# A gated recurrence with its products regrouped: gates and queries transposed by the matmul, values beside the attention's keys, both head pairs in one pass

## The chip, the cores and the metric

The kernel runs on one core of a Trainium2 chip. TensorE (PE in the profile) multiplies matrices out of SBUF into PSUM banks; VectorE (DVE) and ScalarE (ACT) do the elementwise work; GpSimd (POOL) does a little; SyncE (SP) issues most DMAs. The metric is the device time of one execution in microseconds (us); lower is better.

## The reference, cut to what matters

The network is two transformer blocks in fp32 on 256 tokens `x` (and, in the first block, 256 context tokens `ctx`). The first block has two layers, `l = 0` and `l = 1`; each mixes its tokens by a Fourier mix, an attention and the gated recurrence of this change, from one projection `u = h @ w_in`, and then has a feed-forward part. Layer 0 gives outputs for both sequences; layer 1 gives outputs for `x` alone, but still needs the recurrence's states after `ctx`. The recurrence runs forward (gate columns `OFF_FF`) and backward (`OFF_FB`), in chunks of 64 tokens, with 4 heads of 64:

```python
k = (1 - lb) * sigmoid(-z);  log_f = log(lb + (1 - lb) * sigmoid(z))     # per direction
def step(s, inp):                                                        # one chunk
    kc, vc, lf, qc = inp
    cum = cumsum(lf);  last = cum[-1]
    s_new = exp(last) * s + einsum('sd,se->de', kc * exp(last - cum), vc)
    o_inter = einsum('td,de->te', qc * exp(cum), s)
    att = einsum('td,sd,tsd->ts', qc, kc, exp(cum_t - cum_s) where s <= t)
    return s_new, o_inter + einsum('ts,se->te', att, vc)
...
y = rmsnorm(o_forward + o_backward, gain) * silu(g)
```

The second block (windowed and dilated attention, feed-forward) is not touched by the change.

## The kernel before, in words

**Products.** A product in fp32 is made from three fast ones: each operand is split into a high part (`hi`, line 170, on ACT) and the rest (`lo`, line 171, on DVE), and `mm3` issues hi·hi, hi·lo and lo·hi (lines 177 to 179). The weights come by DMA in chunks of two k-tiles (`raw`), and are split into `whi` and `wlo`. `gemm` keeps the activations stationary and streams the weights, so its result has tokens on partitions. `gemm_t` keeps the weights stationary and streams 512 tokens, so its result has columns on partitions, i.e. transposed; `gemm_t2` does this for 256 tokens.

**The recurrence in `mix1`.** The four heads are two pairs, `fd` 0 and 1. `z_(fd)` makes 512 columns for one pair by `gemm`: 128 each of forward gate, backward gate, values and queries, which `hg_load` collects from four places of `w_in` in pieces of 128 columns. The result is copied to `zn`. In layer 1 the context tokens take 384 of the columns (no queries), and `z_(0)` is made in two gemms, for `ctx` and for `x`, each with its own loading and splitting of the weights. `h_(seq, fd)` then does a sequence of 256 tokens (four chunks) for one pair, in one call of `fwd`:

- `hgrn_gates`: PE transposes the gates (line 1102, four transposes) and the queries (line 1115, two) into PSUM; sigmoids from there (lines 1106 and 1107, ACT); products of query and gate (DVE).
- `hgrn_levels`: the attention within a chunk is built in levels of block size 1, 2, 4, ..., 32, after a group for the diagonal. A level copies halves of `hxy` into `hkm` (lines 1184 and 1186, ACT), multiplies 64x64 blocks (line 1156, PE; the profile counts 16 for one pair), and puts the result under a mask into `hatt` (line 1167, `copy_predicated`, DVE). Then DVE multiplies the gates of the level into `hxy` (lines 1202 and 1203), which the next level's copies wait for. So there are 7 groups for a sequence and a pair with queries. A pass without queries (`ctx` in layer 1) has none of these groups.
- `hgrn_states`: transposes of the keys (line 1222), products with the values (line 1235), the running states `hst` (line 1251), and their copies `hsb` (line 1264).
- `hgrn_out`: products of queries with states and of `hatt` with values (lines 1283 and 1293).

Tiles of a pass have two buffers each (`hbufs = 2`). `k_` makes the attention's keys and values, 256 columns for all tokens; `q_`, `g_` and `u_` make queries, the output gate and the Fourier part; `e_` ends a pool; `r_` normalises the recurrence's output; `a_` is the attention. `STEPS` gives the order in which these are written, one string for each layer. A scheduler merges the written instructions into one list per engine, so that a gemm's matmuls lie between the small steps of the recurrence. The first product of layer 0 is started while the norm still runs (`start` in `run`), as its chunks arrive.

Of the kernel before, what the change touches and what calls it, by code (L numbers as in the profile page):

```python
# [12 lines left out]
F32 = mybir.dt.float32  # L13
# [18 lines left out]
    "z0 h00 z1 g h01 e k h10 h11 q u m a r",  # L32
    "z0 h00 h10 z1 e h01 k h11 q g u m a r",
# [61 lines left out]
class Net:  # L95
    def __init__(self, ctx, tc, A, out, taps=None, stop=None):
# [16 lines left out]
        self.hbufs = 2  # L113
# [613 lines left out]
    def gemm_t(self, xT, w, n0, nb, first=False):  # L727


        xh, xl = xT  # L730
# [20 lines left out]
        return acc  # L751
# [336 lines left out]
    def hgrn_gates(self, pool, zn, seq, fds, l, with_q):  # L1088


        nc, nf = self.nc, len(fds)
        f = self.t(pool, [P, 2 * nf, 256], F32, "hf", bufs=self.hbufs)
        xy = self.t(pool, [P, 4 * nf, 256], F32, "hxy", bufs=self.hbufs)
        q = self.t(pool, [P, 2 * nf, 256], F32, "hq", bufs=self.hbufs) if with_q else None
        ends = xy.rearrange("p (s j) t -> p s j t", s=4)[:, 0::3]
        for i in range(2):
            ts = slice(i * P, i * P + P)
            ps = self.tr_bank()
            for j, fd in enumerate(fds):
                for d in range(2):  # L1100
                    o = (d * nf + j) * P
# [253 lines left out]
    def mix1(self, hp, pool, l, hT, start=None, late=None):  # L1355
# [61 lines left out]
        def h_(seq, fd):  # L1417
            with_q = seq in seqs
            now = nexts == f"h{seq}1"
            if now:  # L1420
                obank(seq)
# [493 lines left out]
```

## Time and profile before

| what | value |
|---|---|
| median of 3 runs | 1678.8 us (1677.87 to 1680.21) |
| profiled execution: time | 1683.74 us |
| profiled execution: span | 1681.9 us |
| granted TensorE clock, mean over the span | 0.989 |
| busy share of the span | PE 96%, weight loads 80%, DVE 73%, ACT 51%, POOL 3% |
| DMA | 310.48 MB, mean 185 GB/s |
| chain that ended last, by engine | PE 71%, DVE 10%, DMA 10%, ACT 5%, issue 3% |

The span is the profiled execution without the time around it (1683.74 - 1681.9 = 1.8 us). The recurrence of layer 0 lies in the stretch from 23 to 200 us, that of layer 1 between 700 and 820 us. The chain is followed back from the last instruction; a share of PE in it is time for which nothing but PE's own work was waited for. A busy PE counts overlapping matmuls once, so the cost of a matmul is read from the start of one to the start of the next.

### The profile page before, as it was taken

The page shows a single profiled execution, that of the slowest core. Times are in us where ns is not written, and L with a number is a line of the kernel's source. Part 1 is how long each engine was busy: PE and PEld are TensorE (multiplying, and loading weights), DVE is VectorE, ACT ScalarE, POOL GpSimd, SP SyncE. Part 2 cuts the span into 40 slices and gives each one's busy share as a digit, 9 for nine tenths or more (in the row PEclk, how much of TensorE's full clock was granted, in tenths as well). Part 3 has the DMA queues.
Part 4 walks back from the last instruction along what each step waited for, and adds up shares of the span by engine and source line. Part 5 has one row for each costly group of instructions (what it writes and reads, how often), then busy time and mean ns, then how long its engine had stood idle before and what let it go on. Part 6 is the DMA issues. An engine that isn't in the chain of part 4 may idle for free.

```text
span 1681.9 us, 27316 instructions
## 1 busy us (share of the span) xinstructions
PE 1621.6 (96%) x10343; PEld 1344.0 (80%) x10343; DVE 1222.3 (73%) x2042; ACT 855.5 (51%) x1697; POOL 44.6 (3%) x53
## 2 busy tenths in 40 slices
PE   7999899999999999999999999999999999899998
PEld 5777757878888888787678899777989988779896
DVE  4558866887878977878768897887776567575555
ACT  4446664533333234554755455686454456564443
POOL 0001100000000000101000000000000000000000
PEclk9999999999999999999999999999999999999999
DMA  9550415554678886532258897533876543256653
GB/s 325 187 176 27 161 64 188 176 189 165 212 231 297 271 265 222 161 90 70 91 187 295 309 315 253 158 119 119 275 260 188 185 135 90 85 176 173 206 175 112
DMA packets 169482, 310.48 MB, mean 185 GB/s; under 512 B 12163, under 2 KB 72819, under 8 KB 169350
## 3 DMA queue, kind: packets, MB, share of 16 engines
q1 hardware_dynamic: 168966, 308.17, 56.8%
q8 instruction: 81, 1.33, 0.3%
q10 hardware_dynamic: 384, 0.56, 0.1%
q14 instruction: 51, 0.42, 0.1%
HBM read 307.64 MB, written 1.05 MB: 184 GB/s over the span
## 4 chain that ended last, share of the span: by engine, by line
PE 71%; DVE 10%; DMA 10%; ACT 5%; issue 3%; POOL 1%; SPq 1%; ACTq 0%; POOLq 0%; DVEq 0%
PE bank L179 19%; PE bank L177 19%; PE bank L178 19%; DVE wlo L171 3%; ACT whi L170 3%; PE bank L970 2%; PE bank L897 2%; DMA raw<-ffn_w_in 2%; DMA raw<-w_up 2%; DMA raw<-w_down 2%; DMA raw<-w_gate 1%; PE bank L1512 1%; PE bank L321 1%; DMA raw<-ffn_w_out 1%; PE bank L1156 1%
## 5 line engine op out<-in xcount | busy, mean ns | idle before, releaser
L170 ACT CAST whi<-raw 128x1024 fp32r<-128x1024 f32 (+2 forms) x420 | 401.1, 959 | 525.4 <-PE bank L179 186.6
L171 DVE TENSOR_TENSOR wlo<-raw,whi 128x1024 fp32r<-128x1024 f32 (+2 forms) x420 | 464.7, 1111 | 239.2 <-ACT whi L170 237.2
L177 PE MATMUL bank<-hh,whi 128*128 128x256 f32 (+1 forms) x1240 | 385.4, 311 | 0.0
L178 PE MATMUL bank<-hl,whi 128*128 128x256 f32 (+1 forms) x1240 | 384.8, 311 | 0.0
L179 PE MATMUL bank<-hh,wlo 128*128 128x256 f32 (+1 forms) x1240 | 384.3, 311 | 0.4 <-DVE wlo L171 0.2
L177 PE MATMUL bank<-whi,hh 128*128 128x512 f32 (+2 forms) x720 | 266.8, 374 | 11.0 <-ACT hh L170 5.8
L178 PE MATMUL bank<-wlo,hh 128*128 128x512 f32 (+2 forms) x720 | 265.5, 369 | 2.1 <-DVE wlo L171 2.1
L179 PE MATMUL bank<-whi,hl 128*128 128x512 f32 (+2 forms) x720 | 263.8, 370 | 0.2 <-DVE hl L171 0.2
L179 PEld LDWEIGHTS bank<-hh,wlo 128*128 128x128 f32 x1240 | 233.3, 188 | 16.0 <-DVE wlo L171 1.0
L178 PEld LDWEIGHTS bank<-hl,whi 128*128 128x128 f32 x1240 | 233.7, 188 | 14.8
L177 PEld LDWEIGHTS bank<-hh,whi 128*128 128x128 f32 x1240 | 233.6, 188 | 14.9
L358 DVE SCALAR_TENSOR_TENSOR acc<-adaw,cs,acc 128x1024 f32<-128x1024 f32 x154 | 196.4, 1281 | 20.0 <-DMA adaw<-ada_w 10.8
L178 PE MATMUL bank<-wlo,acth 128*128 128x512 f32 x440 | 173.6, 394 | 0.5 <-DVE wlo L171 0.5
L177 PE MATMUL bank<-whi,acth 128*128 128x512 f32 x440 | 173.3, 394 | 0.0
L179 PE MATMUL bank<-whi,actl 128*128 128x512 f32 x440 | 172.6, 392 | 0.0
L177 PEld LDWEIGHTS bank<-whi,hh 128*128 128x128 f32 x720 | 138.0, 193 | 38.7 <-ACT hh L170 8.0
L179 PEld LDWEIGHTS bank<-whi,hl 128*128 128x128 f32 x720 | 138.5, 192 | 23.7 <-DVE hl L171 3.7
L178 PEld LDWEIGHTS bank<-wlo,hh 128*128 128x128 f32 x720 | 138.6, 193 | 21.9 <-DVE wlo L171 3.4
L177 PEld LDWEIGHTS bank<-whi,acth 128*128 128x128 f32 x440 | 82.7, 188 | 18.8 <-DVE sg L840 0.4
L179 PEld LDWEIGHTS bank<-whi,actl 128*128 128x128 f32 x440 | 82.8, 188 | 18.7
L178 PEld LDWEIGHTS bank<-wlo,acth 128*128 128x128 f32 x440 | 82.7, 188 | 18.7 <-DVE wlo L171 0.9
L756 DVE TENSOR_TENSOR rtmp<-bank,gate 128x512 f32<-128x512 f32 x68 | 46.6, 686 | 32.3 <-PE bank L179 32.3
(297 smaller groups left out, 1834.7 us busy)
## 6 DMA issues: line engine op xcount, KB each, us to landing
adaw<-ada_w SPq DMA_DIRECT2D x96, 512.0 KB
adaw<-w_ada SPq DMA_DIRECT2D x80, 512.0 KB
raw<-ffn_w_in SPq DMA_DIRECT2D x64, 512.0 KB
raw<-w_down SPq DMA_DIRECT2D x46, 512.0 KB
raw<-ffn_w_out SPq DMA_DIRECT2D x40, 512.0 KB
raw<-w_gate SPq DMA_DIRECT2D x32, 512.0 KB
raw<-w_up SPq DMA_DIRECT2D x32, 512.0 KB
raw<-w_in SPq DMA_DIRECT2D x56, 256.0 KB
```

Source lines behind the costliest of these rows:

```text
L170: a = self.nc.scalar.copy(hi, src)
L171: b = self.nc.vector.tensor_sub(lo, src, hi.bitcast(F32))
L177: mm(out, lh, rh, start=start, stop=False)
L178: mm(out, lh, rl, start=False, stop=False)
L179: mm(out, ll, rh, start=False, stop=stop)
L321: nc.tensor.matmul(ps[h][32 * g : 32 * g + 32], self.cs32[:, k0 + g], raws[g][:, h * 512 : h * 512 + 512], start=k0 == 0, stop=k0 > 0,)
L358: nc.vector.scalar_tensor_tensor(acc, raw, s, acc, op0=ALU.mult, op1=ALU.add)
L756: nc.vector.tensor_mul(tmp[:, :nw], ps[:, :nw], gate[:, n0 : n0 + nw])
L897: self.nc.tensor.transpose(ps[:, i * P : i * P + P], ps_in[:, i * P : i * P + P], self.ident)
L970: self.nc.tensor.matmul(o[e * 64 : e * 64 + 64], v, pt[:, e::2, i], start=i == 0, stop=i == len(vs) - 1)
L1156: nc.tensor.matmul(banks[hp][(c % 2) * 64 : (c % 2) * 64 + 64, 2 * j + c // 2], lhs(hs, j, c), rhs(hs, j, c), start=True, stop=True,)
L1512: nc.tensor.matmul(dst, q, ksT[:, i, kv, :nk], start=i == 0, stop=i == 1)
```

## The change

The 512 gate columns of both pairs become one `gemm_t` (`f_`), and the 256 query columns another (`y_`; in layer 1 a `gemm_t2` for `x` alone). Both come out transposed, in `zf` and `zq`, so that the transposes of `hgrn_gates` go. The values join the attention's keys and values in one gemm of 512 columns (`v_`, result `zv`). `hgrn_gates`, `hgrn_levels`, `hgrn_states` and `hgrn_out` now always take both pairs (`nf = 2`), so that an instruction of a level has twice the elements and a group of 64x64 products has 32 instead of 16. The pass is cut in two steps: `L_(seq)` is gates and levels, `S_(seq)` is states and outputs, and other work may be written between them. The tiles of a pass have one buffer (`hbufs = 1`). Line numbers shift: line 1156 becomes 1147, 1167 becomes 1158, 1184 and 1186 become 1175 and 1177, 1202 and 1203 become 1193 and 1194.

```diff
 STEPS = (
-    "z0 h00 z1 g h01 e k h10 h11 q u m a r",
-    "z0 h00 h10 z1 e h01 k h11 q g u m a r",
+    "f y L0 g e v S0 L1 q S1 u m a r",
+    "f L0 e v y S0 L1 q g u S1 m a r",
 )
...
-        self.hbufs = 2
+        self.hbufs = 1
...
+    def gemm_t_steps(self, xT, w, n0, nb, first=False, ahead=0):
...
-    def hgrn_gates(self, pool, zn, seq, fds, l, with_q):
-
-
-        nc, nf = self.nc, len(fds)
+    def hgrn_gates(self, pool, z, qv, l):
+
+
+
+        nc, nf, fds = self.nc, 2, (0, 1)
         f = self.t(pool, [P, 2 * nf, 256], F32, "hf", bufs=self.hbufs)
         xy = self.t(pool, [P, 4 * nf, 256], F32, "hxy", bufs=self.hbufs)
...
-                    nc.tensor.transpose(
-                        ps[:, o : o + P], zn[fd][:, 2 * seq + i, d * P : d * P + P], self.ident
-                    )
...
+        nc.scalar.activation(f, z, AF.Sigmoid)
+        nc.scalar.activation(
+            ends, z.rearrange("p (d j) t -> p d j t", d=2), AF.Sigmoid, scale=-1.0
+        )
...
-    def hg_load(self, l, fd, m):
...
+        def f_():
+
+            z_["f"] = z = self.t(pool, [P, 4, 512], F32, "zf", bufs=1)
+            if start is None:
+                acc = self.gemm_t(hT, w, 1024, 4, first=True)
+            else:
+                *_, acc = start
+            for i, a in enumerate(acc):
+                self.copy(z[:, i], a)
+
+        def y_():
+
+            z_["q"] = z = self.t(pool, [P, 2, 512 if ctx_out else 256], F32, "zq", bufs=1)
+            if ctx_out:
+                for i, a in enumerate(self.gemm_t(hT, w, 1792, 2)):
+                    self.copy(z[:, i], a)
+            else:
+                (a,) = self.gemm_t2(self.sides(hT)[1], w, 1792, 2)
+                self.copy(z, a.rearrange("p (j t) -> p j t", j=2))
...
+        def L_(seq):
+            q = None
+            if seq in seqs:
+                q = z_["q"][:, :, 256 * seq : 256 * seq + 256] if ctx_out else z_["q"]
+            z = z_["f"][:, :, 256 * seq : 256 * seq + 256]
+            f, xy, ks = self.hgrn_gates(hg, z, q, l)
+            att, last = self.hgrn_levels(hg, f, xy, q, ks)
+            kept[seq] = xy, att, last
+
+        def S_(seq):
+            xy, att, last = kept.pop(seq)
+            out = seq in seqs
+            self.hgrn_states(hg, xy, last, z_["v"], seq, states, sbs if out else None)
+            if out:
+                o = self.ac_bank()
                 osb[seq] = self.t(pool, [P, 512], F32, "osb", bufs=len(seqs))
...
-        def k_():
+        def v_():
...
-            acc = self.gemm(hT, range(KT), w, 0, 768, 256, allt)
+            wv = w[:, 768:].rearrange("k (m c) -> k m c", m=2)
+            load = lambda dst, k: nc.sync.dma_start(
+                out=dst.rearrange("p (m c) -> p m c", m=2), in_=wv[k : k + P, :, :256]
+            )
+            acc = self.gemm(hT, range(KT), load, 0, 0, 512, allt)
             for i, a in enumerate(acc):
+                self.copy(zv[:, i], a[:, 256:])
+                self.copy(v[:, i], a[:, 128:256])
...
-            start = self.gemm_steps(
-                hT, range(KT), self.hg_load(0, 0, 4), 0, 0, 512, [0, 128, 256, 384], ahead=1, early=True
-            )
+            start = self.gemm_t_steps(hT, A["w_in"][0], 1024, 4, ahead=1)
```

The first place is PE in layer 1, in the levels of the `x` tokens. Before, three groups of line 1156 stand there with no gemm's matmul between them (each group has its own `hkm`):

```order
L177 MATMUL bank_1514_7932<-whi_7936,hh_6416 128x256
...
L1156 MATMUL bank_1462_7621<-hkm_7617 64x64
...
L1156 MATMUL bank_1465_7640<-hkm_7636 64x64 x4
...
L1156 MATMUL bank_1468_7659<-hkm_7655 64x64
...
L178 MATMUL bank_1483_7797<-wlo_7838,hh_6416 128x512
```

Now four groups of the doubled size (line 1147) stand together, between a matmul with `whi` of a gemm of 256 columns and the one with its `wlo`; each group has 16 of these rows, of which one stands here:

```order
L179 MATMUL bank_1390_7405<-whi_7408,hl_6158 128x256
...
L177 MATMUL bank_1390_7405<-whi_7426,hh_6157 128x256
L1147 MATMUL bank_1346_7164<-hkm_7160 64x64
...
L1147 MATMUL bank_1349_7191<-hkm_7187 64x64
...
L1147 MATMUL bank_1352_7218<-hkm_7214 64x64
...
L1147 MATMUL bank_1355_7245<-hkm_7241 64x64 x3
...
L1213 MATMUL bank_1419_7560<-ident_73,hxy_7069 128x128 x4
L178 MATMUL bank_1389_7404<-wlo_7427,hh_6157 128x256
```

What moved is the gemm work: it stands before and behind the four groups, and one more group, each of 32 instead of 16 products by the profile's count, is in the row.

The second place is DVE in layer 0, in the first two levels of the first pass. Before (`h00`, one pair):

```order
L1202 TENSOR_TENSOR hxy_616<-hxy_616,hf_615 128x256
L1203 TENSOR_TENSOR hxy_616<-hxy_616,hf_615 128x256
L1167 COPY_PREDICATED hatt_636<-mask_546,bank_150_653 128x128
...
L1202 TENSOR_TENSOR hxy_616<-hxy_616,hlev_635 128x128x2
L1203 TENSOR_TENSOR hxy_616<-hxy_616,hlev_635 128x128x2
```

Now (`L0`, both pairs):

```order
L1193 TENSOR_TENSOR hxy_719<-hxy_719,hf_718 128x512
L1194 TENSOR_TENSOR hxy_719<-hxy_719,hf_718 128x512
L1158 COPY_PREDICATED hatt_727<-mask_542,bank_174_752 128x256
...
L1193 TENSOR_TENSOR hxy_719<-hxy_719,hlev_726 128x256x2
L1194 TENSOR_TENSOR hxy_719<-hxy_719,hlev_726 128x256x2
L171 TENSOR_TENSOR wlo_948<-raw_945,whi_947 128x512
```

The kinds and their order are the same; each has twice the elements, and there are half as many of them in a layer.

The third place is ACT in layer 0 between the states of `ctx` (step `S0`) and the levels of `x` (`L1`), in the changed kernel. `hsb` are the states' copies, and the sigmoid into `hxy` writes the one buffer that the outputs of `S0` read:

```order
L1255 COPY hsb_578<-hst_576 64x2x3x64 x2
L1107 ACT_TABLE_LOAD
L1107 ACTIVATE hxy_1463<-zf_582 128x2x512
L1411 COPY osb_1420<-bank_282_1419 128x512
L1175 COPY hkm_1492<-hxy_1463 128x512
L1177 COPY hkm_1492<-hxy_1463 128x256 x2
```

On PE, the last output products of `S0` (line 1284) and the first group of `L1` (line 1147) stand there so:

```order
L1284 MATMUL bank_282_1419<-zv_1123,hatt_727 64x64 x16
L178 MATMUL bank_312_1657<-wlo_1693,hh_112 128x512
L179 MATMUL bank_312_1657<-whi_1692,hl_113 128x512
L177 MATMUL bank_313_1658<-whi_1692,hh_112 128x512
...
L177 MATMUL bank_314_1659<-whi_1692,hh_112 128x512
L178 MATMUL bank_314_1659<-wlo_1693,hh_112 128x512
L1147 MATMUL bank_289_1472<-zq_611,hks_1466 64x64
```

The sigmoid and its table load stand behind the last copy of `S0`, and 10 gemm matmuls of 512 columns stand between the last output product and the first group (5 of them left out here). Before, `hxy` had two buffers, and a pass could begin before the outputs of the one ahead of it were done.

## Rows read from the trace of the kernel before

**Rows 1.** Page, part 1: busy time, share of the span and instructions by engine.
```profile
PE 1621.6 (96%) x10343; PEld 1344.0 (80%) x10343; DVE 1222.3 (73%) x2042; ACT 855.5 (51%) x1697; POOL 44.6 (3%) x53
```

**Rows 2.** Stretches: length, busy time by engine, granted clock, DMA share, GB/s.
```profile
0.00:20.00 20.00, 11.00 (x85) 7.58 (x89) 8.49 (x26) 11.99 (x26) 3.17 (x10) 1.00 0.97 316
100.00:140.00 40.00, 40.00 (x484) 32.10 (x483) 28.97 (x99) 21.46 (x56) 2.82 (x4) 1.00 0.25 77
140.00:180.00 40.00, 38.42 (x497) 28.95 (x496) 32.30 (x100) 21.01 (x58) 5.21 (x3) 0.98 0.22 65
180.00:200.00 20.00, 17.39 (x104) 14.56 (x103) 16.64 (x33) 13.39 (x30) 3.27 (x2) 0.86 0.65 235
779.00:787.00 8.00, 6.17 (x59) 4.51 (x60) 6.40 (x21) 2.36 (x9) 0.00 (x0) 0.57 0.23 67
780.00:800.00 20.00, 17.80 (x200) 14.47 (x201) 15.73 (x42) 8.95 (x22) 2.90 (x2) 0.85 0.33 93
```

**Rows 3.** Timeline of PE, 162.5 to 164.6: start, duration, line, output<-inputs.
```profile
162.96 0.39 PE L177 MATMUL bank<-whi,hh 128*128 128x512 f32 x1
163.28 0.46 PE L1156 MATMUL bank<-hkm 64*64 64x64 f32 x16
163.68 0.51 PE L178 MATMUL bank<-wlo,hh 128*128 128x512 f32 x1
164.02 0.40 PE L179 MATMUL bank<-whi,hl 128*128 128x512 f32 x1
```

**Rows 4.** Timeline of PE, 71.8 to 73.8.
```profile
71.91 0.39 PE L177 MATMUL bank<-whi,hh 128*128 128x512 f32 x1
72.14 0.40 PE L178 MATMUL bank<-wlo,hh 128*128 128x512 f32 x1
72.46 0.74 PE L1235 MATMUL bank<-zn,hkn 64*64 64x64 f32 x32
73.14 0.50 PE L179 MATMUL bank<-whi,hl 128*128 128x512 f32 x1
73.47 0.40 PE L177 MATMUL bank<-whi,hh 128*128 128x512 f32 x1
```

**Rows 5.** Timeline of PE, 150.5 to 155.
```profile
153.57 0.40 PE L178 MATMUL bank<-wlo,hh 128*128 128x512 f32 x1
153.90 0.63 PE L1102 MATMUL bank<-ident,zn 128*128 128x128 f32 x4
154.28 0.48 PE L179 MATMUL bank<-whi,hl 128*128 128x512 f32 x1
```

**Rows 6.** Groups by form, 23 to 200: busy, mean ns; idle before.
```profile
L1186 ACT COPY hkm<-hxy 128x128 f32<-128x128 f32 x48 | 12.5, 300 | 0.7 <-DVE hxy L1203 0.6
L1167 DVE COPY_PREDICATED hatt<-mask,bank 128x128 f32<-128x128 uint32 x48 | 12.1, 299 | 2.1 <-PE bank L1156 1.7
L1156 PE MATMUL bank<-hkm 64*64 64x64 f32 x384 | 11.5, 230 | 0.2 <-ACT hkm L1186 0.2
L1184 ACT COPY hkm<-hxy 128x256 f32<-128x256 f32 x24 | 9.9, 414 | 9.4 <-DVE hxy L1202 6.3 <-DVE hxy L1134 2.5
...
L1202 DVE TENSOR_TENSOR hxy<-hxy,hlev 128x256 f32<-128x256 f32 x20 | 8.4, 422 | 2.1 <-ACT hkm L1184 1.9
...
L1016 DVE TENSOR_TENSOR hxh<-bank,hrstd 128x512 f32<-128x512 f32 x4 | 2.8, 690 | 1.4 <-POOL hrstd L430 1.3
...
L1106 ACT ACT_TABLE_LOAD x2 | 2.6, 1283 | 0.9 <-DVE rsk L1000 0.9
```

**Rows 7.** Waits of PE, 176 to 200: total, times, longest.
```profile
PE bank L1038 <- DVE qnat L171: 2.9, 2, 1.4
PE bank L177 <- DVE hxh L1016: 0.7, 1, 0.7
```

**Rows 8.** Waits of PE, 760 to 800.
```profile
PE bank L1156 <- ACT hkm L1186: 1.2, 1, 1.2
...
PE bank L1156 <- DVE hatt L1167: 0.5, 1, 0.5
```

More of the change, by code (lines that the diff above doesn't have):

```diff
@@ L727, in gemm_t @@
     def gemm_t(self, xT, w, n0, nb, first=False):
+        *_, acc = self.gemm_t_steps(xT, w, n0, nb, first)
+        return acc
+    def gemm_t_steps(self, xT, w, n0, nb, first=False, ahead=0):
         xh, xl = xT
@@ L737, in gemm_t @@
             steps = [(c, slice(s, s + 256)) for s in (0, 256) for c in range(n)] + steps[n:]
+        if ahead:
+            ws[0] = self.weights(w, 0, 2, n0, nb * P)
+            yield acc
         for c, ts in steps:
-            if c not in ws:
-                ws[c] = self.weights(w, 2 * c, 2, n0, nb * P)
-                self.tick()
+            for i in range(c, min(c + 1 + ahead, KT // 2)):
+                if i not in ws:
+                    ws[i] = self.weights(w, 2 * i, 2, n0, nb * P)
+                    self.tick()
             hi, lo = ws[c]
@@ L1380, in mix1 @@
         ps = []
-        def z_(fd):
-            nonlocal start
-            z = self.t(pool, [P, 4, 512], F32, "zn", bufs=2)
-            parts = [(allt, 4)]
-            if not ctx_out:
-                parts = [(allt[:2], 3), (xt, 4)] if fd == 0 else [(allt, (3, 3, 4, 4))]
-            zn.append(z)
-            for toks, m in parts:
-                ms = m if isinstance(m, tuple) else (m,) * len(toks)
-                if start is None:
-                    acc = self.gemm(
-                        hT, range(KT), self.hg_load(l, fd, max(ms)), 0, 0, max(ms) * P, toks,
-                        widths=[n * P for n in ms],
-                    )
-                else:
-                    *_, acc = start
-                    start = None
-                for a, tok, n in zip(acc, toks, ms):
-                    self.copy(z[:, tok // P, : n * P], a[:, : n * P])
+        def f_():
[14 more added lines that the diff above has]
+                self.copy(z, a.rearrange("p (j t) -> p j t", j=2))
         def e_():
@@ L1407, in e_ @@
             ps.append(hes.enter_context(self.tc.tile_pool(name=f"att{l}", bufs=2)))
-        def obank(seq):
-            if seq in seqs and seq not in os_:
-                os_[seq] = self.ac_bank()
-                osb[seq] = self.t(pool, [P, 512], F32, "osb", bufs=len(seqs))
-            return os_.get(seq)
-        kept, nexts = {}, ""
[L1417 to L1421, printed above, removed]
-            xy, att = fwd(seq, (fd,))
-            if not with_q:
-                return
-            kept[seq, fd] = xy, att
-            if now or fd == 1:
-                o = obank(seq)
-                for d in range(2):
-                    if (seq, d) in kept:
-                        xy, att = kept.pop((seq, d))
-                        self.hgrn_out(o, xy, att, zn, seq, (d,), sbs)
-                if fd == 1:
-                    nc.scalar.copy(osb[seq], o)
@@ L1522, in a_ @@
                 self.attention(ps[0], groups, nk // P, nk)
-        fn = dict(z=z_, e=e_, h=h_, H=H_, k=k_, q=q_, u=u_, g=g_, m=m_, r=r_, a=a_)
-        steps = STEPS[l].split()
-        for step, nexts in zip(steps, steps[1:] + [""]):
+        fn = dict(f=f_, y=y_, e=e_, L=L_, S=S_, v=v_, q=q_, u=u_, g=g_, m=m_, r=r_, a=a_)
+        for step in STEPS[l].split():
             fn[step[0]](*map(int, step[1:]))
```

74 lines of the change are left out of this document (20 added, 54 removed).

## The prediction, on record before the changed kernel ran

> **What bounds the kernel now.** I read the page's first part, the busy time by stretches, the timeline of PE at single small steps, the groups of instructions by form, and then what PE waited for, each where the recurrence lies. PE is busy for 1621.6 of 1681.9 us [rows 1], so time is lost or won on PE first of all: by its work, by its waits, and by its clock. The reader is to see three things in the stretches [rows 2]. From 100 to 140 us, in the recurrence of layer 0, PE has no idle time at all, with DVE at 28.97 and ACT at 21.46 of 40: there PE's own work is the bound. From 180 to 200 us, behind it, PE is busy for 17.39 of 20 and the granted clock is 0.86. From 780 to 800 us, in the last pass of layer 1, PE is busy for 17.80 of 20 at 0.85. So the same recurrence is bound by PE in one place and by the elementwise engines in another, and the change has to be priced at each.
>
> **What PE saves.** The products of `w_in` cost the same: the multiplications are regrouped, and the columns that pass through PE are the same number, at 0.23 us for 512 (start to start, 71.91 to 72.14) [rows 4]. Two things do get cheaper.
>
> A group of 16 small products between gemm matmuls: from 162.96 to 164.02 is 1.06 us, in which two gemm matmuls of 0.23 also begin, which leaves 0.60 [rows 3]. A group of 32: from 72.14 to 73.47 is 1.33, less 0.46, is 0.87 [rows 4]. It is a group of line 1235, not of 1156, but of the same 64x64 blocks, so I take it as the price of a merged one. Two of 16 become one of 32: 2 x 0.60 - 0.87 = 0.33 saved. Layer 0 has 4 passes x 7 groups = 28, which become 14: 4.6 us. (The trace counts 384 products with `hkm` there, 24 groups of 16 [rows 6]; 4 more come from the diagonal.) Layer 1 has 14 groups, which become 7: 2.3 us.
>
> Transposes: four of line 1102 cost 153.57 to 154.28 less 0.23, which is 0.48 [rows 5]. Two of line 1115 I take at half, 0.24 (between nothing and 0.48). Layer 0 loses four of each set: 1.9 + 1.0 = 2.9. Layer 1 loses four and two: 1.9 + 0.5 = 2.4.
>
> PE's work is so 7.5 us shorter in layer 0 and 4.7 in layer 1, 12.2 in all.
>
> **What a level now waits for.** In a level, DVE's two products follow ACT's copies, and the next level's copies follow the products. For one pair the copies are 0.414 + 2 x 0.300 and the products 2 x 0.422 [rows 6]: 1.0 + 0.8 = 1.9 us. For both pairs the trace has no such row. DVE's 128x512 product elsewhere takes 0.690 [rows 6]; ACT's copies go up by 0.114 for 128 elements, which gives an estimate of 0.64 for 512 and 0.41 for 256. So 1.46 + 1.38 = 2.84 us. DVE alone has the products and two masked copies, at 0.42 each (between 0.299 as now and twice that; nearest the product of 256 elements): 1.38 + 0.84 = 2.2 us. PE has, by the order of the changed kernel, 6 gemm matmuls of 512 columns (or 12 of 256) between two groups in layer 0: 6 x 0.23 + 0.87 = 2.25 us. If the first copies of a level start while the second product still runs, DVE's 2.2 decides and PE waits for nothing; if nothing overlaps, PE waits 0.6 us in each of 12 levels, 7 us. DVE also has splits of weights in its line, as the order shows. I take 0.25 a level, 3 us, for layer 0, between 0 and 7.
>
> **One buffer.** `L1` of layer 0 can write `hxy` only when `S0` has read it. Behind that stand a table load of 1.283 us [rows 6], a sigmoid of 1024 elements (estimate 1.1, by the same 0.114 for 128) and one product of 0.69: 3.1 us. PE has 10 matmuls there, 2.3 us. I take 0.8 us, between 0 (the table load can be early) and 3.1. In layer 1 the first pass has no outputs to read `hxy`, and I count nothing.
>
> Beside this stands a rule of the Trainium skill ("Perfetto Trace Analysis", Optimization Strategy): a gap that repeats on an engine that should be full can mean that there are too few buffers for the next tile. It speaks against `hbufs = 1`; by it the gap would come at every pass, which is two places in a layer at most, and no run shows it yet.
>
> **Layer 1.** Here the wait that is there grows. Now three groups stand together without a gemm matmul between; PE waits 1.2 us for copies and 0.5 for a masked copy there [rows 8], and with the smaller waits around I count 2.9. The clock granted from 779 to 787 is 0.57 [rows 2], after these waits began: 0.43 x 8 = 3.4 us of full speed lost. In the changed kernel four doubled groups stand together. From one to the next is some 2.5 to 2.84 us (the chain above), of which 0.87 is PE's, so three waits of 1.6 to 2.0, and one split of weights (0.69 at least, the product of the same width) in DVE's line: 3 x 1.8 + 0.7 = 6.1. That is 3.2 more than now. The stretch at half clock becomes longer too; in proportion to the waits it would double, but its end is set by the gemm work that follows, so I take 1.5 us more (between 0 and 3.4). Sum: 4.7 lost against 4.7 saved, nothing for layer 1, between -5 and +8.
>
> The skill's page "TensorE: Matmul & The Clock Gate" (Why this matters for your kernels) says that idle gaps of PE between matmuls bring its clock down to the lower level. The stretch of 0.57, a mix of 1.2 and 2.4 GHz, agrees. By this rule the four doubled groups are where the change would lose.
>
> **Behind the recurrence of layer 0.** PE waits 2.9 + 0.7 us there, for splits of queries and a norm on DVE [rows 7], and 0.14 x 20 = 2.8 us go by the clock. DVE's share gets lighter: a level costs it 2.2 instead of 2 x (0.84 + 0.60) = 2.9 for both pairs, 0.7 x 12 = 8 us less over layer 0. But `S1` now lies after the queries, so that its states compete with the same norms. I take 2 us back, between 0 and 6.
>
> **Start.** In the first 20 us the DMA share is 0.97 [rows 2]. The first chunks now are whole rows of 512 columns and not four pieces. The bytes are the same; I take nothing, and at most 0.8 us, half of what a chunk of 512 KB takes at 316 GB/s.
>
> **Sum.** -7.5 + 3 + 0.8 - 2 in layer 0 and 0 in layer 1: -5.7. On the profiled execution, 1683.7 becomes 1678.0. That execution lies 4.9 us above the median of 1678.8, so the median becomes 1673.1; I say 1673. A measurement of this kernel tells some 0.2%, 3.4 us, from no change: below 1675.4 is faster, above 1682.2 slower.
>
> **Rivals.** *The saving is swallowed.* The levels run at their full chain in layer 0 (+7 for +3), and the tail gives nothing back: -7.5 + 7 + 0.8 + 0 = 0, time 1679. For it speaks that DVE and ACT are nearly as long as PE in a level; against it that copies and products of two pairs overlap in part already now (1.9 us for a pair, and PE did not wait from 100 to 140).
>
> *Slower: the levels go serial.* DVE works in order, and a level's masked copy stands ahead of the next level's products. If PE's group comes late, because it stands behind gemm matmuls or because it waits itself, the masked copy is late, and with it the next products: then copies, group, masked copies and products add up, 1.46 + 0.87 + 0.84 + 1.38 = 4.55 us a level. The point from which it decides is a group that ends later than the level's products, i.e. more than 1.4 us after its copies. In the four groups of layer 1 alone this gives 3 x (4.55 - 0.87) = 11 us of waiting for 2.9, with 3.4 us of clock; with 7 us in layer 0: (-7.5 + 7 + 0.8) + (-4.7 + 8.1 + 3.4) = +7, time 1686. For it: gemm matmuls of 1.4 us stand between groups. Against: before, the same order of copies held PE nowhere in layer 0.
>
> *Faster still: PE bound all through.* No stalls in the levels, and the tail of layer 0 closes: -12.2 - 6 = -18, time 1661. For it: PE's full 40 us of 40. Against: the four groups without a cover.
>
> **Numbers.** My forecast 0.45, with a range of its own from 1668 to 1678; swallowed 0.2, slower 0.2, faster still 0.15. Of mine 0.40 are faster and 0.05 the same; of the swallowed 0.15 the same, 0.02 faster and 0.03 slower; of the serial 0.17 slower and 0.03 the same. Together: faster 0.57, same 0.23, slower 0.20. The range takes in the faster rival and most of the slower: 1660 to 1685.
>
> **What would show it.** In the profile of the changed kernel: PE's busy time some 12 us shorter (more, if its waits' half clock goes; less, if it grows); groups of 32 at 0.87 start to start; levels of layer 0 about 2.5 us apart; PE waits of 1.6 to 2.0 us between the four groups of layer 1 with a clock under 0.6; about 1 us before the first group of `L1` in layer 0; fewer waits from 176 to 200. I am wrong if levels lie 3 us or more apart where gemm matmuls are ready, or if a group of 32 costs two of 16.

## The result, and the profile after

| | before | changed |
|---|---|---|
| median | 1679.5 us (1677.9 to 1684.8, 4 runs) | 1665.0 us (1662.0 to 1666.9, 4 runs) |
| ratio to before | | 0.9899, 95% interval 0.9882 to 0.9916 |
| profiled execution, span | 1681.9 us | 1662.2 us |
| granted clock over the span | 0.989 | 0.994 |

The changed kernel is faster by 1.0% (0.84 to 1.18%), 14 to 20 us of 1679.5. The same kernel run again later (e11) gave 1661.8 us and a ratio of 0.9885 (0.9867 to 0.9903). The page's first part answers to [rows 1]:

```profile
PE 1602.0 (96%) x10275; PEld 1329.9 (80%) x10275; DVE 1208.7 (73%) x1911; ACT 845.3 (51%) x1616; POOL 47.2 (3%) x53
```

PE's busy time is 19.6 us shorter, and as a share of the span it is what it was. The stretches answer to [rows 2], with one of my own choice for the levels of layer 1 (columns as there):

```profile
0.00:20.00 20.00, 11.03 (x84) 7.51 (x88) 8.38 (x26) 11.90 (x26) 3.18 (x10) 1.00 0.96 325
100.00:140.00 40.00, 39.78 (x333) 30.64 (x333) 24.02 (x67) 16.91 (x32) 2.80 (x4) 1.00 0.17 47
140.00:180.00 40.00, 36.50 (x510) 30.26 (x510) 31.89 (x70) 19.72 (x41) 7.02 (x4) 0.96 0.18 49
180.00:200.00 20.00, 19.17 (x121) 14.02 (x120) 18.55 (x42) 17.51 (x50) 5.04 (x2) 1.00 0.71 257
760.00:776.00 16.00, 10.41 (x191) 8.93 (x191) 15.46 (x34) 8.12 (x20) 1.46 (x1) 0.69 0.14 36
780.00:800.00 20.00, 18.75 (x243) 14.78 (x243) 16.36 (x39) 14.53 (x29) 0.00 (x0) 1.00 0.43 139
```

From 180 to 200 us the clock is full now, and PE is busy for 19.17. The place at the groups of layer 1, from 779 to 787 us before [rows 2], lies from 760 to 776 us now and is longer: PE works for 10.41 of 16 at a clock of 0.69.

Where did the time go? I cut both profiles at the same work: at the first DVE product with a gate behind layer 0's mixing, at the second token tile of layer 1's norm, at the first product with a gate behind layer 1's mixing. The four stretches before:

```profile
20.00:266.30 246.30, 240.66 (x2017) 173.60 (x2007) 161.74 (x433) 126.40 (x299) 14.79 (x12) 0.99 0.44 143
266.30:700.30 434.00, 430.11 (x1984) 349.32 (x1983) 353.70 (x412) 182.05 (x380) 8.11 (x7) 1.00 0.67 220
700.30:858.30 158.00, 147.01 (x1175) 114.84 (x1174) 121.40 (x323) 90.64 (x190) 10.81 (x10) 0.96 0.34 107
858.30:1681.90 823.60, 792.84 (x5094) 698.70 (x5092) 576.94 (x849) 444.45 (x805) 7.74 (x14) 0.99 0.60 190
```

And in the changed kernel:

```profile
20.00:257.60 237.60, 231.93 (x1946) 166.79 (x1939) 155.95 (x360) 120.86 (x252) 16.70 (x12) 0.99 0.43 146
257.60:693.10 435.50, 431.33 (x2001) 350.32 (x1999) 354.78 (x413) 182.46 (x379) 8.39 (x7) 1.00 0.67 221
693.10:842.40 149.30, 138.06 (x1163) 109.14 (x1163) 113.20 (x265) 84.20 (x155) 10.95 (x10) 0.97 0.30 92
842.40:1662.20 819.80, 789.69 (x5092) 696.18 (x5090) 576.37 (x850) 445.93 (x805) 7.95 (x14) 1.00 0.60 192
```

Layer 0's mixing is 8.7 us shorter, and layer 1's 8.7 us. The code between them and behind them is unchanged, and +1.5 and -3.8 us there come from the spread of single executions: in the profiles of the experiments below, those stretches take 432.7 to 436.4 and 817.4 to 821.7 us. The 823.6 of before lies above that, as the execution does: it was 4.2 us above its median. In both layers PE's idle time, length less busy, is as before: 5.6 and 5.7 us in layer 0, 11.0 and 11.2 in layer 1. So all of it came out of busy time.

Busy time holds work and clock. The granted clock at any moment of these stretches is 1 (2.4 GHz) or 0.5 (1.2 GHz). If PE's busy time at 0.5 counts half, an estimate of its work at full speed is left (us; the last rows are of experiments told below):

| | length | idle | busy | of it at 0.5 | work |
|---|---|---|---|---|---|
| layer 0, before | 246.3 | 5.6 | 240.7 | 6.7 | 237.3 |
| layer 0, changed | 237.6 | 5.7 | 231.9 | 3.4 | 230.2 |
| layer 1, before | 158.0 | 11.0 | 147.0 | 11.9 | 141.0 |
| layer 1, before, in e5 | 156.5 | 11.6 | 144.9 | 6.2 | 141.8 |
| layer 1, changed | 149.3 | 11.2 | 138.1 | 6.4 | 134.9 |
| e1, layer 0 and 1 | 240.6, 155.5 | 3.6, 14.0 | 237.0, 141.5 | 0, 9.8 | 237.0, 136.6 |
| e7, layer 0 and 1 | 237.1, 154.2 | 3.4, 11.4 | 233.7, 142.8 | 0, 11.0 | 233.7, 137.3 |

Layer 0 lost 7.1 us of work and layer 1 6.2, or 7.0 against e5's profile, in which layer 1 is that of before. The rest is clock: half speed cost PE by this estimate 3.4 us before and 1.7 now in layer 0, and 6.0 and 3.2 in layer 1. Of layer 1's 6.0, 3.4 fell on 704.3 to 707.7 and 847.6 to 851.0 us; e5's profile has full speed at both ends of that layer, so those 3.4 do not belong to the change.

The prices of a level can now be read and not only estimated. Groups by form in layer 0, 20 to 200 us:

```profile
L1158 DVE COPY_PREDICATED hatt<-mask,bank 128x256 f32<-128x256 uint32 x24 | 9.4, 447 | 0.9 <-PE bank L1147 0.9
...
L1177 ACT COPY hkm<-hxy 128x256 f32<-128x256 f32 x24 | 8.8, 415 | 0.0
...
L1175 ACT COPY hkm<-hxy 128x512 f32<-128x512 f32 x12 | 7.7, 640 | 6.4 <-PE bank L1147 6.2
...
L1193 DVE TENSOR_TENSOR hxy<-hxy,hlev 128x512 f32<-128x512 f32 x10 | 6.8, 685 | 0.0
```

A 512-wide copy takes 0.640 us (estimate 0.64), a 256-wide one 0.415 (0.41), a product 0.685 (0.69), a masked copy 0.447 (0.42). A group of 32 small products on PE's timeline, in layer 1:

```profile
758.28 0.39 PE L179 MATMUL bank<-whi,hl 128*128 128x512 f32 x1
758.60 0.70 PE L1147 MATMUL bank<-hkm 64*64 64x64 f32 x32
759.23 0.51 PE L177 MATMUL bank<-whi,hh 128*128 128x512 f32 x1
759.58 0.40 PE L178 MATMUL bank<-wlo,hh 128*128 128x512 f32 x1
```

From 758.28 to 759.58 is 1.30, less two gemm matmuls of 0.23, which is 0.84 us: I had 0.87.

### The profile page after: what moved, and what is told of

It reads as the page before. It is cut to its first block, busy times and chain, and to the rows that moved or that the text cites. A ratio compares the mean times of both kernels' runs of the same rounds, so it can differ in the third digit from the quotient of the medians.

```text
span 1662.2 us, 26872 instructions
## 1 busy us (share of the span) xinstructions
PE 1602.0 (96%) x10275; PEld 1329.9 (80%) x10275; DVE 1208.7 (73%) x1911; ACT 845.3 (51%) x1616; POOL 47.2 (3%) x53
## 4 chain that ended last, share of the span: by engine, by line
PE 72%; DVE 9%; DMA 8%; ACT 6%; issue 3%; POOL 1%; SPq 0%; ACTq 0%; POOLq 0%; DVEq 0%
PE bank L177 20%; PE bank L179 20%; PE bank L178 20%; DVE wlo L171 3%; ACT whi L170 3%; PE bank L980 2%; PE bank L907 2%; DMA raw<-w_up 2%; DMA raw<-w_in 1%; DMA raw<-w_gate 1%; DMA raw<-w_down 1%; PE bank L321 1%; PE bank L1483 1%; PE bank L1048 1%; DMA raw<-w_out 1%
## 5 line engine op out<-in xcount | busy, mean ns | idle before, releaser
L171 DVE TENSOR_TENSOR wlo<-raw,whi 128x1024 fp32r<-128x1024 f32 (+2 forms) x416 | 460.7, 1112 | 253.0 <-ACT whi L170 249.7
L177 PE MATMUL bank<-hh,whi 128*128 128x256 f32 (+1 forms) x1360 | 426.4, 314 | 0.0
L179 PE MATMUL bank<-hh,wlo 128*128 128x256 f32 (+1 forms) x1360 | 424.7, 313 | 0.9 <-DVE wlo L171 0.9
L178 PE MATMUL bank<-hl,whi 128*128 128x256 f32 (+1 forms) x1360 | 425.2, 313 | 0.0
L178 PEld LDWEIGHTS bank<-hl,whi 128*128 128x128 f32 x1360 | 256.6, 189 | 17.2
L177 PE MATMUL bank<-whi,hh 128*128 128x512 f32 (+2 forms) x592 | 221.3, 377 | 9.1 <-ACT hh L170 6.7
L178 PE MATMUL bank<-wlo,hh 128*128 128x512 f32 (+2 forms) x592 | 220.1, 373 | 0.5 <-DVE wlo L171 0.4
L179 PE MATMUL bank<-whi,hl 128*128 128x512 f32 (+2 forms) x592 | 217.8, 372 | 0.2 <-DVE hl L171 0.2
L177 PEld LDWEIGHTS bank<-whi,hh 128*128 128x128 f32 x592 | 111.2, 189 | 33.2 <-ACT hh L170 9.1
L179 PEld LDWEIGHTS bank<-whi,hl 128*128 128x128 f32 x592 | 112.1, 189 | 22.0 <-DVE hl L171 4.0
L178 PEld LDWEIGHTS bank<-wlo,hh 128*128 128x128 f32 x592 | 112.2, 190 | 19.4 <-DVE wlo L171 1.5
```

The lines of the kernel that those rows point to most:

```text
L171: b = self.nc.vector.tensor_sub(lo, src, hi.bitcast(F32))
L177: mm(out, lh, rh, start=start, stop=False)
L178: mm(out, lh, rl, start=False, stop=False)
L179: mm(out, ll, rh, start=False, stop=stop)
```

## The experiments

All ratios are to the kernel before, measured beside it; 0.1% is 1.7 us, and a difference to the changed kernel is the difference of two ratios unless medians are named. By whole times only e1, e2, e3 and e8 lie outside both intervals of the changed kernel; the others are read from the layers. "Layer 0" and "layer 1" are the stretches of mixing cut as above, the first counted from the program's start: 257.6 and 149.3 us in the changed kernel, 257.0 and 149.3 in its second profile. Where an experiment leaves a layer's code alone, layer 0 took 257.2 and 258.1 us (e4, e5) and layer 1 149.9 to 150.5 (e3, e8, e12): differences under some 1.2 us say nothing.

**e1_pairs: the levels unmerged.**

```diff
+        for j in range(nf):
+            cur = self.pair_levels(
+                pool, f[:, j::2], xy[:, j::2], lev[:, j::2],
...
-                kq = self.t(pool, [P, 2 * nf, 256], F32, "hkm", bufs=self.hbufs)
+                kq = self.t(pool, [P, 2 * nf, 256], F32, "hkm", bufs=2)
```

> The changed kernel with its levels split again into the two pairs (groups of 16 products, copies and products of half the width, twice as many); gates, queries, values and the order of the steps stay as changed. Theory A (the gain is PE's own work, merged groups 6.9 us and transposes 5.3 us of it): PE gets 4.6 us more in layer 0 and 2.3 in layer 1, so 5 to 7 us over the changed kernel, near 1671. Theory B (merging gives nothing, because each level's copies and products double with it; the gain is in waits and clock behind the recurrence): within 2 us of the changed kernel or below it, 1661 to 1667, with no wait of PE over 1 us at the levels.

The edit also gives `hkm`, the tile of ACT's copies, two buffers. Measured: 1673.8 us, ratio 0.9966 (0.9952 to 0.9981), 11 us over the changed kernel (8.7 by the medians).

```profile
20.00:260.60 240.60, 237.01 (x1951) 167.01 (x1951) 161.64 (x427) 124.69 (x288) 16.55 (x12) 1.00 0.43 144
697.00:852.50 155.50, 141.54 (x1161) 111.01 (x1162) 117.80 (x316) 86.27 (x173) 11.40 (x11) 0.96 0.29 90
```

Layer 0 is 3.0 us longer although the wait that the changed kernel has at 150.7 us (below) is not in this profile, layer 1 6.2. Theory B falls. Theory A has the direction, and its size is too small: by the table PE has 6.8 us more work in layer 0 and 1.8 in layer 1, 8.6 where I had 6.9. The rest is waiting and clock: in layer 1, 10 of the 14 small groups then stand together without a gemm matmul, PE is idle for 14.0 us, and half speed lasts from 770.5 to 784.2 us.

**e2_old_merged: the levels merged on the old columns.** The kernel before has a step for both pairs at once.

```diff
-    "z0 h00 z1 g h01 e k h10 h11 q u m a r",
-    "z0 h00 h10 z1 e h01 k h11 q g u m a r",
+    "z0 z1 H0 g e k H1 q u m a r",
+    "z0 z1 H0 e k H1 q g u m a r",
...
-        self.hbufs = 2
+        self.hbufs = 1
```

> The kernel before with its own step for both pairs in one pass (H0, H1: levels merged, one buffer), but products and transposes as before. It does the other half of the change alone. Theory A: the groups' 6.9 us are saved, the transposes' 5.3 us are not, and some waits at merged levels come in: 1670 to 1675. Theory B: as before, 1677 to 1682.

Measured: 1686.7 us, ratio 1.0031 (1.0009 to 1.0054), slower than before. Both expectations miss.

```profile
702.90:864.80 161.90, 143.10 (x1174) 114.75 (x1174) 117.85 (x270) 86.62 (x162) 10.68 (x10) 0.96 0.32 101
```

In layer 1 PE is idle for 18.8 us of 161.9, where before had 11.0 of 158.0; PE's busy time fell by 3.9 us, and the waits took more than that. Merging the levels alone is a loss in this order of steps. The edit changes three things at once, the merge, the order (`z1` now ahead of the first levels) and the buffers (one for two); which of them brings the waits is not shown.

**e3_no_cover0: layer 0's first levels without a gemm beside them.** (`u` moves ahead of `S1` with it.)

```diff
-    "f y L0 g e v S0 L1 q S1 u m a r",
+    "f y L0 e v S0 L1 q g u S1 m a r",
```

> The changed kernel with the gates' gemm of layer 0 written later, behind the values and L1 (f y L0 e v S0 L1 q g u S1), so that five groups of the first pass of layer 0 stand on PE without a gemm matmul between them. Theory A with my chain of 2.5 to 2.8 us a level: five waits of 1.6 to 2.0 us, and half clock on top, so 8 to 12 us over the changed kernel, 1673 to 1677. Rival (the chain is short, because copies and products overlap across levels): under 1 us a level, 3 us or less in all, under 1669.

Measured: 1673.2 us, ratio 0.9962 (0.9946 to 0.9978); layer 0 takes 265.8 us, 8.2 more. The timeline of PE in that pass:

```profile
70.63 0.69 PE L1147 MATMUL bank<-hkm 64*64 64x64 f32 x32
71.25 2.37 PE L321 MATMUL bank<-adaw,cs 128*32 128x512 f32 x14
73.55 0.69 PE L1147 MATMUL bank<-hkm 64*64 64x64 f32 x32
74.18 1.90 PE L321 MATMUL bank<-adaw,cs 128*32 128x512 f32 x4
76.01 0.69 PE L1147 MATMUL bank<-hkm 64*64 64x64 f32 x32
```

The groups lie 2.9 and 2.5 us apart, near the chain of 2.5 to 2.84. PE's weight loads wait for ACT's copies there, 4.2 us at five groups between 58 and 82 us. But the profile calls none of it idle on PE: products with `adaw` (line 321) run meanwhile, 14 of them for 2.37 us and 4 for 1.90. At 61.23 us, where no group stands between, 16 of them took 1.92: four at a time, at 61.23, 61.68, 62.11 and 62.54. The four between the groups are a single chain with the same steps, at 74.18, 74.63, 75.06 and 75.49. So PE was busy for 20.0 us of 20 and got less done. The size was right; the half clock that I expected with it did not come (1.00 from 60 to 80 us).

**e4_cover1: layer 1's cover moved to the last levels.**

```diff
-    "f L0 e v y S0 L1 q g u S1 m a r",
+    "f L0 e v S0 y L1 q g u S1 m a r",
```

> The changed kernel with the queries' product of layer 1 written behind S0 (f L0 e v S0 y L1 q g u S1), so that three of the four last groups of layer 1 have 1.4 us of gemm matmuls between them, and two of the first ones none. Theory A: waits of 1.4 to 1.5 us at three groups go, two of some 1.5 us come, the half clock falls on less: 1 to 4 us under the changed kernel, 1661 to 1664. Rival (the wait only moves to the place that has lost its cover): within 1 us of the changed kernel, 1664 to 1666.

Measured: 1665.1 us, ratio 0.9913 (0.9885 to 0.9941); layer 1 takes 151.2 us, 1.9 more. The rival is right: the waits moved to the first groups (1.5 us twice), and mostly gemm matmuls behind them ran at the lower clock: from 760 to 770 us PE was busy for 10.00 of 10 at a clock of 0.75. That this place is dearer for it is not shown: 1.9 us hardly stand out of the spread.

**e5_layer0_only: layer 1 as before, layer 0 as changed** (old functions kept beside the new ones).

```diff
-            mT = self.mix1(hp, pool, 1, hT)
+            mT = self.mix1_old(hp, pool, 1, hT)
```

> Layer 0 as changed, layer 1 as before (old steps, columns per pair, transposes, two buffers). Profiles show both layers' stretches 8.7 us shorter in the changed kernel. Theory A (each layer's gain is its own, layer 1's from less work and from gemm matmuls that no longer run at half clock there): the stretch of layer 1 is again 156 to 159 us instead of 149.4, the whole 7 to 9 us over the changed kernel. Rival (layer 1's gain is a chance of one profiled execution, and is near the nothing that I forecast): within 3 us of the changed kernel, and the layer's stretch no longer than 153.

Measured: 1667.7 us, ratio 0.9934 (0.9910 to 0.9957), 6 to 8 us over the changed kernel.

```profile
20.00:258.10 238.10, 231.95 (x1950) 166.99 (x1943) 156.00 (x363) 120.94 (x252) 16.68 (x12) 0.99 0.43 146
693.00:849.50 156.50, 144.91 (x1174) 112.45 (x1174) 121.15 (x323) 89.86 (x188) 10.82 (x10) 0.98 0.34 104
```

Layer 0 stays as changed, layer 1 goes back to 156.5 us. Theory A holds: each layer's gain is its own, and layer 1's 7 us are no chance.

**e6_no_pool: the power on GpSimd left out.**

```diff
-        nc.vector.tensor_scalar(r, ss, 1.0 / width, EPS, op0=ALU.mult, op1=ALU.add)
-        nc.gpsimd.tensor_tensor(r, r, self.mhalf[:, :n], op=ALU.pow)
+        nc.vector.tensor_scalar(r, ss, 0.0, 0.125, op0=ALU.mult, op1=ALU.add)
```

It came from this place in the changed kernel, the second pass of layer 0 (DVE, GpSimd and PE, in order of time):

```profile
147.56 0.17 DVE L429 TENSOR_SCALAR hrstd<-hss 128x8 f32<-128x8 f32 x1
...
147.87 1.64 POOL L430 TENSOR_TENSOR hrstd<-hrstd,mhalf 128x8 f32<-128x8 f32 x1 [22.37 <-DVE hrstd L429]
...
149.54 0.69 DVE L1026 TENSOR_TENSOR hxh<-bank,hrstd 128x512 f32<-128x512 f32 x1 [1.81 <-POOL hrstd L430]
150.15 0.76 DVE L1158 COPY_PREDICATED hatt<-mask,bank 128x256 f32<-128x256 uint32 x2
...
150.73 0.92 PE L1147 MATMUL bank<-hkm 64*64 64x64 f32 x32 [1.89 <-DVE hatt L1158]
...
151.58 0.79 PE L177 MATMUL bank<-whi,hh 128*128 128x512 f32 x1
...
152.17 0.63 PE L178 MATMUL bank<-wlo,hh 128*128 128x512 f32 x1
...
152.60 0.63 PE L179 MATMUL bank<-whi,hl 128*128 128x512 f32 x1
```

A norm of the queries starts its power on GpSimd at 147.87. DVE's next instruction is the norm's product, which waits 1.81 us for it; behind that stands a level's masked copy, and PE's next group waits 1.89 us for the bank which that copy reads. Then gemm matmuls start 0.43 us apart (152.17 to 152.60) where 0.23 is usual: the granted clock is 0.5 from 151.6 to 155.0 us, 0.91 over 140 to 160.

> The changed kernel with the reciprocal root of the head norms and of the recurrence's norm replaced by a constant, made by the same DVE instruction: GpSimd's power is left out there, so the output is not the reference's; order of PE, DVE and ACT unchanged. It takes away what DVE waits for when a norm's product stands ahead of a level's masked copy. Theory A (that wait holds the masked copy, the masked copy PE's next group, and the half clock follows): the wait of 1.9 us at 150.7 and the half clock behind it go, 3 to 6 us under the changed kernel. Rival (levels are bound by DVE's own work, the wait only shows where DVE is behind anyway): 1 us or less.

Measured: 1658.6 us, ratio 0.9883 (0.9853 to 0.9912); layer 0 takes 253.0 us, 4.6 less, layer 1 148.9. By the stretch theory A holds: PE is busy for 19.85 us from 140 to 160, at full clock. By whole times it is not shown: the ratio is 2.7 us under the first of the changed kernel and 0.3 under the second, with overlapping intervals.

**e7_transposes: as many transposes put back.**

```diff
+        for j in range(2):
+            for i in range(2):
+                ps = self.tr_bank()
+                for d in range(2):
+                    nc.tensor.transpose(
+                        ps[:, d * P : d * P + P], z[:, 2 * d + j, i * P : i * P + P], self.ident
+                    )
...
```

> The changed kernel with as many transposes put back on PE as the change took away (four for gates and two for queries, for each pair and sequence), from zf and zq into the same banks, read by nobody. Theory A: their price is 0.48 and 0.24 us a set, 5.3 us in all, 4 to 7 us over the changed kernel. Rival (they lay in the shadow of waits at the start of a pass): 2 us or less.

Measured: 1667.0 us, ratio 0.9923 (0.9898 to 0.9948), 4 to 6 us over the changed kernel.

```profile
20.00:257.10 237.10, 233.67 (x1978) 168.92 (x1979) 156.06 (x364) 120.63 (x253) 16.40 (x12) 1.00 0.43 147
693.30:847.50 154.20, 142.75 (x1183) 113.86 (x1184) 114.09 (x266) 84.28 (x155) 12.40 (x10) 0.96 0.29 89
```

The whole is as expected, though its interval overlaps those of the changed kernel. The layers seem not to be: layer 1 takes 4.9 us more, and layer 0 0.5 less. By the table the work is: 3.4 us more in layer 0 and 2.4 in layer 1, where I had 2.9 and 2.4. In layer 0 the wait of 1.89 us and the half clock behind it are not in this profile, which hides the price; layer 1 has another 3.4 us at half speed at its start, which adds to it.

**e8_u_first: another product beside the second pass.**

```diff
-    "f y L0 g e v S0 L1 q S1 u m a r",
+    "f y L0 g e v S0 L1 u q S1 m a r",
```

> The changed kernel with layer 0's Fourier product written ahead of the attention's queries (L1 u q S1 in place of L1 q S1 u), so that the second pass has gemm matmuls of u beside it and not the norms of the queries. Theory A: the norms no longer stand in DVE's line among the levels, the wait of 1.9 us and its half clock go, 3 to 5 us under the changed kernel; the norms come later, where the attention waits for them, which may cost up to 4 back. Rival (norm work only moves): within 1.5 us of the changed kernel or above it.

Measured: 1669.1 us, ratio 0.9942 (0.9920 to 0.9964); layer 0 takes 262.2 us, 4.6 more. Waits of PE from 165 to 200 us:

```profile
PE bank L1048 <- DVE qnat L171: 4.5, 4, 1.6
```

The wait at the level went (PE is busy for 19.69 us from 140 to 160), and 4.5 us of waits for the queries came where the changed kernel has 1.5 from 170 to 200. The rival holds, and more: the norms moved to a place where PE waits for them longer.

**e11, e9, e12: the norm's sum one tile ahead.** The changed kernel again, and with the sums of squares issued one token tile ahead, in both layers (e9) or layer 0 alone (e12).

```diff
...
+            ahead = stats(0)
-            for a, tok in zip(acc, outt):
+            for n, (a, tok) in enumerate(zip(acc, outt)):
                 i = tok // P
-                q = self.head_norm(ps[0], a, 8, "q", i - 2 if i >= 2 else None)
+                r, ahead = ahead, stats(n + 1) if n + 1 < len(acc) else None
+                with self.tc.issue_after(self.last_sum):
+                    q = self.head_norm(ps[0], a, 8, "q", i - 2 if i >= 2 else None, r)
```

> The changed kernel itself, beside the next two on one chip, as the number that they are compared with: 1661 to 1667 by its first runs.

> The changed kernel with the same arithmetic, but the queries' norms one token tile apart: the sum of squares of tile n+1 is issued ahead of tile n's product with the reciprocal root, so that DVE has a level's masked copies to do while GpSimd makes the power. Theory A (DVE's wait for GpSimd, in order, ahead of a masked copy, costs the second pass of layer 0 a wait of 1.9 us and the half clock behind it): both go, the output stays the reference's, 2 to 5 us under the changed kernel on the same chip. Rival (the norm is late then, and PE waits for the queries instead): within 1 us.

> The stats of the queries one tile ahead in layer 0 alone; layer 1 in the order of the changed kernel. With the norms ahead in both layers, the stretch of layer 0 was 254.2 us against 257.0, and that of layer 1 was 151.9 against 149.3. Theory A (the first is the wait on GpSimd, the second the later norms of layer 1, each by its own layer): 254 and 149.4, so 3 to 6 us under the changed kernel by the ratio to the kernel before, 0.985 or less. Rival (layer 1's difference is the spread of executions): the same as with both, 0.9865.

Measured: on one chip the changed kernel 1661.8 us (1659.8 to 1664.6, ratio 0.9885) and e9 1659.1 (1656.8 to 1660.5, ratio 0.9865, 0.9846 to 0.9883); on another, later, e12 1659.5 (1657.8 to 1661.1, ratio 0.9871, 0.9848 to 0.9893). In e9:

```profile
20.00:254.20 234.20, 230.66 (x1952) 166.00 (x1952) 155.74 (x362) 120.88 (x252) 16.29 (x12) 1.00 0.43 148
140.00:160.00 20.00, 19.87 (x296) 15.04 (x294) 17.95 (x40) 12.10 (x26) 6.49 (x4) 1.00 0.14 42
686.90:838.80 151.90, 140.07 (x1168) 110.37 (x1167) 113.88 (x266) 84.09 (x156) 11.31 (x10) 0.97 0.29 91
```

From 140 to 160 us PE is busy for 19.87 at full clock, where the changed kernel has 0.91; layer 0 takes 2.8 us less than the 257.0 of e11, and 254.4 us in e12. So the cause of that wait is shown: the wait goes with the order of DVE's instructions, the arithmetic being the same. Layer 1 took 151.9 us in e9 and 150.5 in e12, where its order is that of the changed kernel, so a part of that difference at least is spread, and theory A of e12 (0.985 or less) is not reached. Both versions lie some 2.5 us under the changed kernel by the medians; the intervals of the ratios overlap, so a gain of 0.15% in the whole time is likely and not shown.

**e10_levels_late: levels next to states again.**

```diff
-    "f y L0 g e v S0 L1 q S1 u m a r",
-    "f L0 e v y S0 L1 q g u S1 m a r",
+    "f y g e v L0 S0 L1 S1 q u m a r",
+    "f e v y L0 S0 L1 S1 q g u m a r",
```

> The changed kernel with levels and states of a pass next to each other and behind the values (f y g e v L0 S0 L1 S1, and f e v y L0 S0 L1 S1 in layer 1), as in the kernel before, where a pass was one step. Theory A (the levels want gemm matmuls beside them, and writing L ahead of the values is what gives L0 its cover): PE waits grow in both layers, 4 to 10 us over the changed kernel, as in the merged pass on the old columns. Rival (the scheduler finds cover wherever the steps are written): within 2 us.

Measured: 1665.6 us, ratio 0.9909 (0.9890 to 0.9928), 3.8 us over the changed kernel on the same chip by the medians; the intervals overlap. All of it is in layer 0 (260.8 us against 257.0); layer 1 takes 149.3 us. Theory A has the direction and layer 0, and is wrong for layer 1: there the scheduler placed the levels as in the changed kernel, with the same waits of 1.4 to 1.5 us between the last four groups.

## Why the prediction was right, and by what it was too small

The time lies in the range, on the forecast side. That range was wide, 1660 to 1685, and took in rivals on both sides; my own forecast's, 1668 to 1678, does not hold 1665. I had -5.7 us and the change gave some -17 (-14 to -20). By the steps of the prediction:

*What PE saves*, -12.2: holds, and is a little small. By the table it is 7.1 in layer 0 (7.5) and 6.2 to 7.0 in layer 1 (4.7), 13.3 to 14.1 in all. Transposes put back give 5.9 us of work (5.3), unmerged levels 8.6 (6.9).

*Levels of layer 0*, +3 between 0 and 7: right in size and wrong in kind. Levels with gemm matmuls beside them lie 2.2 us apart (groups at 70.1, 72.4, 74.6 and 76.8 us), so copies and products overlap and PE waits for nothing, the lower bound of my range. What came is one wait of 1.89 us with half clock for 3.4 us behind it (1.7 us), from a norm's power on GpSimd, which the sum didn't have. That this came near 3 is luck.

*One buffer*, +0.8: nothing at the place where I counted it. PE has no wait at the first group of `L1`. But one buffer shows in the levels, where I did not look. ACT's copies of a level now wait until PE's group of the level before has read `hkm`, 6.2 us in layer 0 (line 1175 above); with two buffers they waited mostly for DVE's products [rows 6]. Beside gemm matmuls this holds PE nowhere; at the groups of layer 1 without a cover it does:

```profile
767.45 1.36 PE L1147 MATMUL bank<-hkm 64*64 64x64 f32 x32 [1.54 <-DVE hatt L1158]
...
768.94 0.62 ACT L1175 COPY hkm<-hxy 128x512 f32<-128x512 f32 x1 [1.67 <-PE bank L1147]
...
770.22 1.15 PE L1147 MATMUL bank<-hkm 64*64 64x64 f32 x32 [1.41 <-ACT hkm L1177]
```

The copy waits 1.67 us for the group, and the next group 1.41 us for the copies. DVE's product that this copy also needs had ended at 768.21 us (line 1193, 767.53 and 0.68), so some 0.7 us of the wait is the buffer's own, an estimate. The repeated gap that the Trainium skill ("Perfetto Trace Analysis", Optimization Strategy) lets one look for with too few buffers agrees with these waits. Two buffers for `hkm` with merged levels were not tried, so what they would save stays open.

*Behind layer 0*, -2 between 0 and -6: nearly -5, a mis-sized term. PE's waits for queries, a norm and the softmax were 2.9 + 0.7 us [rows 7] and are 1.5 + 0.7 from 170 to 200 us now, 1.4 less. Half speed from 178.6 to 182.0 and from 185.4 to 188.9 us is gone, with PE busy for 3.40 and 3.31 of it: by the estimate 3.4.

*Layer 1*, 0: this is the step that failed. I had 4.7 of work saved and 4.7 lost to waits and clock; the work came, and next to nothing was lost. Waits of PE in layer 1 (700 to 858 us before, 693 to 842 in the changed kernel), first before:

```profile
PE bank L178 <- DVE wlo L171: 2.1, 3, 1.2
PE bank L177 <- ACT whi L170: 1.6, 2, 1.4
PE bank L1512 <- DVE uf L166: 1.4, 1, 1.4
```

And in the changed kernel:

```profile
PE bank L1147 <- ACT hkm L1177: 3.1, 3, 1.4
PE bank L1147 <- DVE hatt L1158: 1.5, 1, 1.5
...
PE bank L177 <- ACT hh L170: 0.9, 1, 0.9
...
PE bank L178 <- DVE wlo L171: 0.4, 1, 0.4
```

At the groups PE waits 4.6 us, against 1.7 before [rows 8]: +2.9, where I had +3.2. Each wait is shorter than my 1.6 to 2.0, at most 1.54. But I counted only this place. For split weights and the Fourier part behind the recurrence PE waited 2.1, 1.6 and 1.4 us before; of these 0.4 is left, and 0.9 for another split. So PE's idle time in the layer stayed as it was (11.2 us, against 11.0 and, in e5, 11.6). What took those waits away is not shown. DVE is 8 us lighter here (121.40 and 113.20 us), but `S1` is also written behind `u` now. And in e10, with the layer as short and DVE as light, 1.4 and 0.5 us of waits for split weights are there, with `S1` written ahead of `u`.

The clock, +1.5, is the other half. Half speed at the groups, before, in e5 and in the changed kernel:

```profile
779.40:786.20 6.80, 5.13 (x54) 3.60 (x49) 5.20 (x16) 2.11 (x7) 0.00 (x0) 0.50 0.20 53
773.20:780.00 6.80, 6.19 (x42) 4.36 (x33) 5.17 (x13) 1.38 (x6) 0.00 (x0) 0.50 0.27 78
766.00:776.20 10.20, 6.40 (x81) 5.66 (x82) 9.66 (x20) 3.77 (x9) 0.00 (x0) 0.50 0.13 33
```

The stretch did become longer, by 3.4 us. But PE is busy for 6.40 us of it, against 5.13 and 6.19: by the estimate 0.1 to 0.6 us more, because much of it is waiting. The rule of the Trainium skill that idle gaps bring the clock down ("TensorE: Matmul & The Clock Gate", Why this matters for your kernels) agrees: half speed begins at 766.0 us, behind waits of 0.28 and 1.43. That the change would lose by it does not follow, since what the clock costs depends on what PE has to do then. So against e5 layer 1 is 7.2 us shorter: 7.0 by work and 0.4 by idle time, with 0.1 lost by the clock. Against before's profile it is 8.7: 6.2 of work and 2.8 of clock (3.4 from the two half-speed stretches at the layer's ends, less 0.6 at the groups), with 0.2 lost in idle time.

*Rivals.* Swallowed: no. Serial levels: not at their 4.55 us, not even without cover (2.1 to 2.8 us a level at 761 to 770 us, and 2.5 to 2.9 in e3). "Faster still" named the right mechanism in layer 0, with PE bound and the tail closed, and its time of 1661 is nearer than my 1673. My reason against it, the four groups without a cover, was true, and the layer gained all the same.

## What to carry to other kernels

When two half-width passes are merged, price the chain of one level at the new width, and look at the waits in the rest of the stretch too: here 2.9 us of new waits at the groups left PE's idle time as it was. Merged steps want other work beside them: the same kernel without it in one pass lost 8.2 us (e3), and the merge on the old columns was a loss (e2). Before a tile goes from two buffers to one, look at who writes it next and whether PE can wait for that. A long operation on a third engine in the middle of a queue that is worked off in order holds all that stands behind it (1.81 us on DVE here): issue its input one tile ahead.

## What was not expected of the hardware

PE can be busy all the time and do a quarter of what it could: a chain of four products with weights 32 wide took 1.90 us in e3, and sixteen, four such chains side by side, 1.92 (61.23 us of the same run). A granted clock of half speed costs little where PE mostly waits: 10.2 us of it in layer 1 held 6.40 us of PE's work, and 6.8 us of it with the old layer (e5) held 6.19.
